# Modulation products on four 32-column strips of the array, partial rows added by a 128x2 matrix or by VectorE

## Chip, cores and metric

One core of one Trainium2 chip. The metric is device microseconds of one execution of the whole program.

## The reference

Two layers of one mixer block over 2048 latent tokens and 256 context tokens, width 1024. Each layer first makes its modulation: `silu(c) @ w_mod + b_mod`, with `w_mod` of 1024 x 3072, cut into shift, scale and gate; the same with `c_ctx` for the context tokens. Then

```
u = standardize(x) * (1 + scale) + shift
heads: latent attention (8), retention (4), gated convolution, all from u @ w_in
x_new = layer_norm(ALPHA * x + gate * (heads @ w_out))
```

Only the products with `w_mod` are touched here. They have two rows (`c` and `c_ctx`), so each is a (2 x 1024) by (1024 x n) product in plain fp32.

## The kernel before

The program writes its order out by hand: every engine call goes through a `Meter` (line 85, which is why the profile gives L85 nearly everywhere) that adds an estimated cost to that engine's planned time, `spent`. Background generators do their next piece when the planned time of PE has passed that of what they wait for (`wait`, line 124). `p_cost` (line 105) charges an fp32 matmul four cycles a column, but one cycle where its output has 32 rows; it was written so for the sums of the softmax denominators (`den_head`, line 1528), four matmuls with a 128x32 matrix of ones whose outputs lie in partitions 0, 32, 64 and 96 of one bank. So what the meter charges sets the order of the program in the stages run by generators; in the attention stage the work is hung on step numbers instead (`later`).

Each layer has three stages: the projections (`stage_in`, line 404), attention (`Attention.run`), and the output (`Output.run`). The attention loop has 576 steps (32 query blocks of 18 key tiles) of six matmuls of 512 columns: three for the scores, one for the maxima of a later block, two for probabilities times values; VectorE reduces the maxima and takes a difference per step, ScalarE makes an exponential and a copy, and GpSimd adds two tiles every second step.

A modulation product has these parts. `mod_load` (247) loads 1024 x n of `w_mod` in four transfers. `mod_mm` (252) runs eight matmuls, k = 0 to 7, with the 128x2 slice of `cT` as the stationary operand and n columns of `wm` moving, all accumulating in partitions 0 and 1 of one bank; each fp32 matmul appears in the trace as two passes. `mod_rows` (261) copies the two rows to SBUF by ScalarE, or for the gate adds the bias by VectorE and stores to `gate_s`. `mod_cols` (269) turns the rows of shift and scale into columns with one PE transpose per 128, and adds the bias.

The products are made in three places:

- **Start, layer 0** (line 1107 on): four products of 512 columns for shift and scale, one after the other with their copies and transposes. Unit 0 (256 tokens) cannot be modulated before the fourth. The generators `gen_x` (standardize units of x), `gen_w` (split weights in two parts) and `gen_u` (modulate and split a unit) are stepped between them.
- **Attention, layer 0** (lines 1603 to 1625): twelve products of 256 columns, one per 40 steps: four for layer 0's gate, eight for layer 1's shift and scale, the latter followed three steps later by `mod_cols`.
- **Change of layers** (`Start.gen_gate`, 391): four products of 256 columns for layer 1's gate, from tiles `wg`; then the second pool of the projection stage is laid over the memory of `wg` (line 414), and units of x are loaded into it. `gen_gate` of `stage_in` (555) adds the bias.

Of the kernel before, what the change touches and what calls it, by code (L numbers as in the profile page):

```python
# [10 lines left out]
F32 = mybir.dt.float32  # L11
F32R = mybir.dt.float32r
I32 = mybir.dt.int32
AF = mybir.ActivationFunctionType
ALU = mybir.AluOpType
AX = mybir.AxisListType
# [3 lines left out]
D = 1024  # L20
# [53 lines left out]
def tile_hybrid(ctx: ExitStack, tc: tile.TileContext, I: dict, out: bass.AP, stop: str = ""):  # L74
    nc = tc.nc
# [41 lines left out]
    V, S, G = Meter(nc.vector, v_cost), Meter(nc.scalar, s_cost), Meter(nc.gpsimd, g_cost)  # L117
    PE, SY = Meter(nc.tensor, p_cost), Meter(nc.sync, d_cost)
# [5 lines left out]
    def wait(*ms):  # L124
        at = max(m if isinstance(m, float) else m.spent for m in ms) + margin["engine"]
        if SY in ms or isinstance(ms[0], float):
            at += margin["dma"]
        yield
        while PE.spent < at:
            yield  # L130


    def pool(name, bufs=1, **kw):
        return tc.tile_pool(name=name, bufs=bufs, reuse_waits="tile", **kw)

    ctx.enter_context(tc.manual_schedule())
    const = ctx.enter_context(tc.tile_pool(name="const", bufs=1))
# [6 lines left out]
    tiny = Tiny()  # L144
# [14 lines left out]
    def ps_o():  # L159
        return next_bank("O", 6, 2)  # L160

    ident = const.tile([128, 128], F32, name="ident")
    make_identity(nc, ident)
    identr = const.tile([128, 128], F32R, name="identr")
    V.tensor_copy(identr, ident)
    ones32 = const.tile([128, 32], F32, name="ones32")
    V.memset(ones32, 1.0)
    idx = const.tile([128, 4], F32, name="idx")
# [2 lines left out]
    def transpose(o, i, n=128, f32r=False):  # L171
        PE.transpose(o, i, (identr if f32r else ident)[0:n, 0:n])
# [9 lines left out]
            V.scalar_tensor_tensor(r, t, 1.5, r, op0=ALU.add, op1=ALU.mult)  # L182
        return r

    cT = const.tile([128, 8, 2], F32, name="cT")
    t_pool = ctx.enter_context(ExitStack())
    crow = t_pool.enter_context(pool("crow")).tile([16, 128], F32, name="crow")
    SY.dma_start(crow[0:8, :], I["c"].rearrange("b (k p) -> (b k) p", p=128))
# [1 line left out]
    if True:  # L190
        cps = ps_o()
        transpose(cps[:, 0:16], crow, 16)
        S.activation(cT.rearrange("p k j -> p j k"), cps[:, 0:16].rearrange("p (j k) -> p j k", j=2), AF.Silu)

    t_pool.close()
    x_s = dram.tile([T, D], F32, name="x_s")
# [8 lines left out]
    L = [dict() for _ in range(DEPTH)]  # L205
# [18 lines left out]
    def mod_params(l, prm):  # L224
        d = L[l]
        prmT = const.tile([128, NPRM], F32, name=f"prmT{l}")

        def rows(r, n, src):
            SY.dma_start(prm[r:r + n, :], src)

        rows(PB_MOD, 24, I["b_mod"][l].rearrange("(k p) -> k p", p=128))
        rows(PG_Q, 2, I["mla_q_norm"][l].rearrange("(k p) -> k p", p=128))
        rows(PG_KV, 1, I["mla_kv_norm"][l].rearrange("(k p) -> k p", p=128))
        rows(PDW, 62, I["conv_dw"][l].rearrange("t (k p) -> (t k) p", p=128))
        rows(PDW_B, 2, I["conv_dw_b"][l].rearrange("(k p) -> k p", p=128))
        rows(PLN_G, 2, I["conv_ln_g"][l].rearrange("(k p) -> k p", p=128))
        rows(PLN_B, 2, I["conv_ln_b"][l].rearrange("(k p) -> k p", p=128))
        rows(PPW_B, 2, I["conv_pw_b"][l].rearrange("(k p) -> k p", p=128))
        d["prm"] = prmT
        d["modc"] = const.tile([128, 16, 2], F32, name=f"modc{l}")  # L240

    def mod_flip(l, prm, p=None):
        p = ps_a() if p is None else p
        transpose(p[:, 0:NPRM], prm[0:NPRM, :], NPRM)
        V.tensor_copy(L[l]["prm"], p[:, 0:NPRM])

    def mod_load(l, c0, n, wm):
        for q in range(4):
            SY.dma_start(wm[:, 2 * q:2 * q + 2, 0:n], I["w_mod"][l, q * 256:(q + 1) * 256, c0:c0 + n]
                         .rearrange("(k p) c -> p k c", p=128))  # L250

    def mod_mm(l, c0, n, wm, ps):
        d = L[l]
        for k in range(8):
            PE.matmul(ps[0:2, 0:n], lhsT=cT[:, k, :], rhs=wm[:, k, 0:n], start=(k == 0), stop=(k == 7))

    def mod_bias(l, c0, n, row):
        if c0 >= 2 * D:
            SY.dma_start(row[:, 0:n], I["b_mod"][l:l + 1, c0:c0 + n].to_broadcast([2, n]))

    def mod_rows(l, c0, n, ps, row):
        if c0 < 2 * D:
            S.copy(row[:, 0:n], ps[0:2, 0:n])
        else:
            V.tensor_tensor(row[:, 0:n], ps[0:2, 0:n], row[:, 0:n], op=ALU.add)
            SY.dma_start(L[l]["gate_s"][:, c0 - 2 * D:c0 - 2 * D + n], row[:, 0:n])
        return row

    def mod_cols(l, c0, n, row, ps):
        d = L[l]  # L270
        nj = n // 128
        mv = ps[:, 0:2 * nj].rearrange("p (c j) -> p c j", j=2)
        for j in range(nj):
            transpose(mv[:, j, :], row[:, j * 128:(j + 1) * 128], 2)
        cs = slice(c0 // 128, c0 // 128 + nj)
        mo = d["modc"][:, cs, :]
        V.tensor_tensor(mo, mv, d["prm"][:, cs, None].to_broadcast([128, nj, 2]), op=ALU.add)
        if c0 >= D:
            V.tensor_scalar(mo, mo, 1.0, None, op0=ALU.add)
# [75 lines left out]
    class Start:  # L355
# [35 lines left out]
        def gen_gate(self, pend):  # L391
            for i in range(2):
                while pend or not (self.PB if i == 0 else self.PS).free:
                    yield
                ps = (self.PB if i == 0 else self.PS).take()
                for j in range(2):
                    c0 = 512 * i + 256 * j
                    mod_mm(self.l, 2 * D + c0, 256, self.wms[2 * i + j], ps[:, c0 % 512:c0 % 512 + 256])
                self.gates.append((512 * i, ps, self.PB if i == 0 else self.PS))
# [4 lines left out]
    def stage_in(l, only, pre):  # L404
# [13 lines left out]
        def slots(n, shape, name, dt=F32, p=keep):  # L418
            return Slots([p.tile(shape, dt, name=f"{name}{i}") for i in range(n)])
# [15 lines left out]
        T2 = slots(6, [128, 2, UN], "t")  # L435
# [118 lines left out]

        def gen_gate(c0, ps, home):
            rt = yield from T2.grab()
            row = rt[0:2].rearrange("p a b -> p (a b)")
            mod_bias(l, 2 * D + c0, 512, row)
            yield from wait(SY)
            mod_rows(l, 2 * D + c0, 512, ps, row)  # L560
            home.put(ps)
            yield from wait(SY)
            T2.put(rt)
# [532 lines left out]
        def idle():  # L1096
            PE.spent += 1000
            sync()
            bg.step()
            pump()  # L1100
# [8 lines left out]
        if l == 0:  # L1109
            with ExitStack() as tmp:  # L1110
                wmp = tmp.enter_context(pool("wm_first"))
                wms = [wmp.tile([128, 8, 512], F32, name=f"wm{i}") for i in range(4)]
                pt = T2.take()
                prm = pt.rearrange("p a b -> p (a b)")[:, 0:128]
                for i in range(4):
                    mod_load(0, i * 512, 512, wms[i])
                    if i == 0:
                        mod_params(0, prm)
                        PE.spent = SY.spent + DMA_LATENCY
                        bg.step()  # L1120
                bg.add(gen_w(wlist))
                bg.add(gen_u(pre.units))
                bg.step()
                rows = [None] * 4
                for i in range(5):
                    if i > 0:
                        mod_cols(0, (i - 1) * 512, 512, rows[i - 1], ps)
                        PB.put(ps)
                    if i < 4:
                        ps = PB.take()  # L1130
                        mod_mm(0, i * 512, 512, wms[i], ps)
                        if i == 0:
                            p = PB.take()
                            mod_flip(0, prm, p)
                            PB.put(p)
                            T2.put(pt)
                        rows[i] = mod_rows(0, i * 512, 512, ps, T2.free[i].rearrange("p a b -> p (a b)")[0:2])
                    idle()
            ready["mod"] = True
        else:  # L1140
            for a in pre.gates:
                bg.add(gen_gate(*a))
            bg.add(gen_w(wlist))
            bg.add(gen_u(pre.units))
# [167 lines left out]
    class Attention:  # L1312
# [96 lines left out]
        def run(self, outer):  # L1409
            l, d, its, state, last = self.l, self.d, self.its, self.state, self.last  # L1410
# [18 lines left out]
            start = {}  # L1429
# [175 lines left out]
            wms, rows = {}, {}  # L1605

            def mod_a(j):
                wms[j] = wmp.tile([128, 8, 256], F32, tag="wm", name="wm")
                mod_load(*mods[j], 256, wms[j])
                rows[j] = tiny.tile([2, 256], F32, tag="row", name="row")  # L1610
                mod_bias(*mods[j], 256, rows[j])

            def mod_b(j):
# [33 lines left out]
            for i in range(len(its)):  # L1647
# [9 lines left out]
                h, b = divmod(i, 4)  # L1657
# [34 lines left out]
            for n in range(-LA, tot):  # L1692
# [16 lines left out]
                if n >= 0:  # L1709
                    i, k = steps[n]  # L1710
# [562 lines left out]
```

## Time and profile before

| | |
|---|---|
| median of 3 runs | 3977.7 us (3975.3 to 3978.64) |
| the profiled execution | 3976.88 us |
| its span | 3974.8 us, granted TensorE clock 0.966 |
| PE, PEld | 93%, 78% of the span |
| VectorE (DVE), ScalarE (ACT), GpSimd (POOL) | 79%, 54%, 60% |

The span is cut out of an execution that took 2.1 us more. Busy shares are means over unlike stages, so the stage in which a product lies is looked at by itself. Overlapping matmuls count as busy PE once; what a group costs PE is read from the start of its first matmul to the start of the next that follows it.

### The profile page before, as it was taken

How to read it: one execution, taken by the hardware profiler on the slowest of the kernel's cores; microseconds unless marked ns; L12 is line 12 of the kernel's file. 1: busy time of each engine (PE TensorE's matmuls, PEld its weight loads, DVE VectorE, ACT ScalarE, POOL GpSimd, SP SyncE). 2: the span in 40 equal slices, each digit the busy share in tenths (PEclk: the TensorE clock that was granted, in tenths of full speed). 3: DMA queues.
4: the chain of work that ended last, by engine and by line, in shares of the span. 5: the costliest groups of instructions: out<-in, count | busy, mean ns of one | idle time of the engine just before them, and what ended most of it. 6: DMA issues, size and time to landing. Idle time of an engine off the chain costs nothing. (4 is left out here: it accounts for less than half of the span.)

```text
span 3974.8 us, 61355 instructions
## 1 busy us (share of the span) xinstructions
PE 3713.1 (93%) x21291; PEld 3106.9 (78%) x21291; DVE 3128.4 (79%) x6455; ACT 2141.5 (54%) x4090; POOL 2377.5 (60%) x1381
## 2 busy tenths in 40 slices
PE   7999988989999999989987999899899999999898
PEld 4999888967777777767767998898777777776676
DVE  4966937978888888868787659558798999998787
ACT  2342323257878877855323333222488888888332
POOL 2455345459988877733333454454499988887333
PEclk9999999989999999999998999999899999999999
DMA  4474543643332212055453653535522322111553
GB/s 155 126 218 118 159 146 105 191 113 83 75 82 63 70 45 53 22 143 161 139 172 104 184 160 115 179 98 175 146 52 60 72 57 50 39 30 44 143 159 109
DMA packets 413466, 438.57 MB, mean 110 GB/s; under 512 B 47850, under 2 KB 364380, under 8 KB 410980
## 3 DMA queue, kind: packets, MB, share of 16 engines
q1 hardware_dynamic: 413156, 434.67, 38.6%
q8 instruction: 167, 2.74, 0.3%
q14 instruction: 143, 1.17, 0.1%
HBM read 293.89 MB, written 140.67 MB: 109 GB/s over the span
## 5 line engine op out<-in xcount | busy, mean ns | idle before, releaser
L85 POOL TENSOR_TENSOR acc<-acc,ph 128x1024 f32<-128x1024 f32 x448 | 1060.5, 2367 | 121.7 <-ACT ph L85 99.2
L85 PE MATMUL bank<-qt,kt 96*128 96x512 f32 (+1 forms) x3456 | 1007.6, 400 | 8.6 <-DVE pl L85 7.3
L85 DVE TENSOR_REDUCE mx<-bank 128x1 f32<-128x512 f32 (+1 forms) x1152 | 787.0, 686 | 196.5 <-PE bank L85 139.8
L85 PEld LDWEIGHTS bank<-qt,kt 96*128 96x128 f32 (+1 forms) x3456 | 655.3, 191 | 229.3 <-issue 17.2
L85 DVE TENSOR_TENSOR pl<-bank,ph 128x512 fp32r<-128x512 f32 x1152 | 783.2, 680 | 28.4 <-ACT ph L85 22.7
L85 ACT ACTIVATE bank<-bank 128x512 f32<-128x512 f32 x1160 | 681.4, 587 | 87.7 <-PE bank L85 79.3
L85 ACT CAST ph<-bank 128x512 fp32r<-128x512 f32 x1152 | 674.7, 586 | 65.3 <-POOL acc L85 3.5
L85 PE MATMUL bank<-w,u 128*128 128x256 f32 (+1 forms) x4224 | 559.5, 290 | 9.1 <-POOL w L85 3.8
L85 PEld LDWEIGHTS bank<-w,u 128*128 128x128 f32 x4224 | 539.2, 193 | 13.6 <-POOL w L85 5.6
L85 PE MATMUL bank<-u,w 128*128 128x256 f32 x4080 | 524.2, 287 | 21.9 <-ACT w L85 9.8
L85 PEld LDWEIGHTS bank<-u,w 128*128 128x128 f32 x4080 | 505.6, 193 | 28.3 <-ACT w L85 10.2
L85 POOL TENSOR_TENSOR w<-x,w 128x512 fp32r<-128x512 f32 (+2 forms) x206 | 342.1, 1679 | 240.7 <-ACT w L85 220.8
L85 PE MATMUL bank<-kt,qt 96*128 96x512 f32 (+1 forms) x1280 | 463.3, 382 | 19.7 <-DMA kt<-k_s 14.4
L85 PE MATMUL bank<-ph,vt 128*128 128x512 f32 x1152 | 460.6, 400 | 1.6 <-ACT o L85 1.6
L85 DVE SCALAR_TENSOR_TENSOR ac<-wn,prmT,ac 128x384 f32<-128x384 f32 (+1 forms) x780 | 456.4, 656 | 0.0
L85 PE MATMUL bank<-pl,vt 128*65 128x512 f32 x1152 | 434.5, 395 | 6.6 <-DVE pl L85 5.5
L85 PE MATMUL bank<-wo,oh 128*128 128x512 f32 x1632 | 416.6, 408 | 9.7 <-DVE wraw L85 9.0
L85 PEld LDWEIGHTS bank<-wo,oh 128*128 128x128 f32 x1632 | 311.1, 196 | 78.7 <-DVE wraw L85 9.5
L85 PEld LDWEIGHTS bank<-kt,qt 96*128 96x128 f32 x1280 | 245.4, 192 | 86.3 <-issue 14.7
L85 POOL TENSOR_TENSOR t<-t,t 128x512 f32<-128x512 f32 x64 | 85.0, 1328 | 340.7 <-DVE t L85 249.5
L85 POOL TENSOR_TENSOR acc<-ph 128x1024 f32<-128x1024 f32 x64 | 151.4, 2366 | 204.3 <-ACT ph L85 200.4
L85 PEld LDWEIGHTS bank<-ph,vt 128*128 128x128 f32 x1152 | 217.2, 189 | 53.9 <-ACT o L85 12.8
(257 smaller groups left out, 4453.7 us busy)
## 6 DMA issues: line engine op xcount, KB each, us to landing
x<-in_w_in_dram SPq DMA_DIRECT2D x106, 512.0 KB
q_s<-so SPq DMA_DIRECT2D x102, 256.0 KB
k_s<-so SPq DMA_DIRECT2D x72, 256.0 KB
v_s<-so SPq DMA_DIRECT2D x36, 512.0 KB
kt<-k_s SPq DMA_DIRECT2D x32, 576.0 KB
vt<-v_s SPq DMA_DIRECT2D x48, 384.0 KB
ret_s<-t SPq DMA_DIRECT2D x70, 256.0 KB
qt<-q_s SPq DMA_DIRECT2D x64, 256.0 KB
```

Of the source, the lines that this page charges most:

```text
L85: return f(*a, **k)
```

## The change

```diff
+    identr = const.tile([128, 128], F32R, name="identr")
+    with ExitStack() as once:
+        eye = once.enter_context(pool("eye")).tile([128, 128], F32, name="eye")
+        make_identity(nc, eye)
+        V.tensor_copy(identr, eye)
+    ident = identr.bitcast(F32)
...
-    cT = const.tile([128, 8, 2], F32, name="cT")
+    cT = const.tile([128, 46], F32, name="cT")
+    V.memset(cT, 0.0)
+    fold = const.tile([128, 2], F32, name="fold")
+    V.tensor_reduce(fold, ident.rearrange("p (j c) -> p c j", c=32)[:, 0:2, :], axis=AX.X, op=ALU.add)
...
         for k in range(8):
-            PE.matmul(ps[0:2, 0:n], lhsT=cT[:, k, :], rhs=wm[:, k, 0:n], start=(k == 0), stop=(k == 7))
+            j = k % 4
+            PE.matmul(ps[32 * j:32 * j + 32, 0:n], lhsT=cT[:, 2 * k:2 * k + 32], rhs=wm[:, k, 0:n], start=(k < 4), stop=(k >= 4))
...
         if c0 < 2 * D:
-            S.copy(row[:, 0:n], ps[0:2, 0:n])
+            S.copy(row[:, 0:n], ps[:, 0:n])
         else:
-            V.tensor_tensor(row[:, 0:n], ps[0:2, 0:n], row[:, 0:n], op=ALU.add)
-            SY.dma_start(L[l]["gate_s"][:, c0 - 2 * D:c0 - 2 * D + n], row[:, 0:n])
+            for j in range(4):
+                V.tensor_tensor(row[0:2, 0:n], ps[32 * j:32 * j + 2, 0:n], row[0:2, 0:n], op=ALU.add)
+            SY.dma_start(L[l]["gate_s"][:, c0 - 2 * D:c0 - 2 * D + n], row[0:2, 0:n])
...
-            transpose(mv[:, j, :], row[:, j * 128:(j + 1) * 128], 2)
+            PE.matmul(mv[:, j, :], lhsT=row[:, j * 128:(j + 1) * 128], rhs=fold, start=True, stop=True)
```

Products k and k + 4 go to strip k % 4 of the array, that is to partitions 32j to 32j + 31 of the bank. The stationary operand is 32 columns wide: the two of this k, and after them those of later k or zeros, so that rows 2 to 31 of a strip hold values that nobody wants. `fold` has a one at partitions 0, 32, 64, 96 in its first column and at 1, 33, 65, 97 in its second: a matmul with it as the moving operand picks the eight good rows, adds the four strips and turns them into columns at once. For the gate four VectorE adds do that. The tiles that hold the rows have all 128 partitions now. The fp32 identity becomes a view of the rounded one, and its own tile a short-lived one. The meter's rule for 32 output rows now also takes `mod_mm`, so that a product is planned at a quarter of its former cost.

## Rows read from the trace of the kernel before

**Rows 1.** Busy time by stretch: stretch, its length, busy us of each engine, granted clock, DMA share, GB/s.

```profile
0.00:50.00 50.00, 35.70 (x102) 10.08 (x102) 15.41 (x52) 5.78 (x11) 0.95 (x7) 1.00 0.70 255
860.00:1660.00 800.00, 798.61 (x3565) 589.11 (x3564) 692.50 (x1130) 645.20 (x1160) 671.00 (x342) 1.00 0.25 61
940.00:980.00 40.00, 40.00 (x180) 28.39 (x179) 33.26 (x54) 31.36 (x57) 38.51 (x24) 1.00 0.38 87
2040.00:2140.00 100.00, 74.01 (x408) 58.97 (x407) 69.75 (x177) 33.77 (x66) 29.89 (x19) 0.84 0.48 153
```

**Rows 2.** Groups of PE matmuls by shape: the products of the attention stage.

```profile
L85 PE MATMUL bank<-wm,cT 128*2 128x256 f32 x192 | 43.4, 379 | 0.0
```

**Rows 3.** Timeline, PE: one product of the attention stage (start us, us).

```profile
1152.97 0.40 PE L85 MATMUL bank<-pl,vt 128*65 128x512 f32 x1
1153.30 3.62 PE L85 MATMUL bank<-wm,cT 128*2 128x256 f32 x16
1156.84 0.96 PE L85 MATMUL bank<-qt,kt 97*128 97x512 f32 x3
```

**Rows 4.** Timeline, PE: the four denominator sums of one head.

```profile
953.26 0.39 PE L85 MATMUL bank<-pl,vt 128*65 128x512 f32 x1
953.57 0.63 PE L85 MATMUL bank<-da,ones 128*32 128x512 f32 x3
...
954.03 0.60 PE L85 MATMUL bank<-da,ones 128*32 128x512 f32 x3
...
954.57 0.73 PE L85 MATMUL bank<-qt,kt 97*128 97x512 f32 x2
```

**Rows 5.** Instructions on the gate's row tile, VectorE (ns min/median/max).

```profile
L85 DVE TENSOR_TENSOR row<-bank,row x4: 411/412/413, 912.6 to 1096.5; 2x256 f32<-2x256 f32 x4
```

**Rows 6.** Timeline, PE: two transposes of a row; full-height fp32 matmuls of 64 columns.

```profile
1161.60 0.28 PE L85 MATMUL bank<-ident,row 2*128 2x2 f32 x2
1161.82 0.97 PE L85 MATMUL bank<-qt,kt 97*128 97x512 f32 x3
...
1721.67 0.39 PE L85 MATMUL bank<-r_st,qT 128*128 128x64 f32 x2
1721.89 0.39 PE L85 MATMUL bank<-rr,am 128*128 128x64 f32 x2
```

**Rows 7.** Timeline of the start.

```profile
1.19 0.36 SPq L85 DMA_DIRECT2D crow<-in_c_dram  x1
...
1.33 0.29 DVE L85 CAST identr<-ident 128x128 fp32r<-128x128 f32 x1 [1.33 <-POOL ident masks.py:199]
...
15.14 8.67 PE L85 MATMUL bank<-wm,cT 128*2 128x512 f32 x16
...
33.27 1.29 DVE L85 BATCH_NORM_STATS2 bs<-so 128x6 f32<-128x512 f32 x2
...
49.45 2.80 ACT L85 ACTIVATE t<-bank,modc 128x256 f32<-128x256 f32 x6
...
52.71 1.08 PE L85 MATMUL bank<-u,w 128*128 128x256 f32 x7
...
63.36 13.97 POOL L85 TENSOR_TENSOR u<-t,u 128x512 fp32r<-128x512 f32 x8 [5.89 <-DVE u L85]
```

**Rows 8.** DMA rates from 0 to 60 us in 40 slices of 1.5 us.

```profile
GB/s 0 31 265 396 324 340 396 351 34 40 339 393 396 396 388 386 389 389 381 389 399 404 382 348 381 407 128 11 0 0 0 0 0 5 165 381 153 0 0 0
```

**Rows 9.** Timeline of the change of layers.

```profile
2069.16 14.31 PE L85 MATMUL bank<-wg,cT 128*2 128x256 f32 x64
...
2080.05 0.79 SPq L85 DMA_DIRECT2D so<-x_s  x2
...
2090.03 0.45 PE L85 MATMUL bank<-ident,so 128*128 128x128 f32 x1 [6.55 <-DVE so L85]
...
2091.12 1.27 DVE L85 TENSOR_TENSOR t<-bank,t 2x512 f32<-2x512 f32 x2
```

**Rows 10.** Waits of SP's queue from 2050 to 2095 us: us, times, longest.

```profile
SPq L85 <- PE bank L85: 4.0, 1, 4.0
```

More of the change, by code (lines that the diff above doesn't have):

```diff
@@ L160, in ps_o @@
         return next_bank("O", 6, 2)
-    ident = const.tile([128, 128], F32, name="ident")
-    make_identity(nc, ident)
     identr = const.tile([128, 128], F32R, name="identr")
-    V.tensor_copy(identr, ident)
+    with ExitStack() as once:
[3 more added lines that the diff above has]
+    ident = identr.bitcast(F32)
     ones32 = const.tile([128, 32], F32, name="ones32")
@@ L192, in tile_hybrid @@
         transpose(cps[:, 0:16], crow, 16)
-        S.activation(cT.rearrange("p k j -> p j k"), cps[:, 0:16].rearrange("p (j k) -> p j k", j=2), AF.Silu)
+        S.activation(cT[:, 0:16].rearrange("p (k j) -> p j k", j=2), cps[:, 0:16].rearrange("p (j k) -> p j k", j=2), AF.Silu)
     t_pool.close()
@@ L254, in mod_mm @@
         for k in range(8):
-            PE.matmul(ps[0:2, 0:n], lhsT=cT[:, k, :], rhs=wm[:, k, 0:n], start=(k == 0), stop=(k == 7))
+            j = k % 4
+            PE.matmul(ps[32 * j:32 * j + 32, 0:n], lhsT=cT[:, 2 * k:2 * k + 32], rhs=wm[:, k, 0:n], start=(k < 4), stop=(k >= 4))
     def mod_bias(l, c0, n, row):
         if c0 >= 2 * D:
-            SY.dma_start(row[:, 0:n], I["b_mod"][l:l + 1, c0:c0 + n].to_broadcast([2, n]))
+            SY.dma_start(row[0:2, 0:n], I["b_mod"][l:l + 1, c0:c0 + n].to_broadcast([2, n]))
     def mod_rows(l, c0, n, ps, row):
         if c0 < 2 * D:
-            S.copy(row[:, 0:n], ps[0:2, 0:n])
+            S.copy(row[:, 0:n], ps[:, 0:n])
         else:
-            V.tensor_tensor(row[:, 0:n], ps[0:2, 0:n], row[:, 0:n], op=ALU.add)
-            SY.dma_start(L[l]["gate_s"][:, c0 - 2 * D:c0 - 2 * D + n], row[:, 0:n])
+            for j in range(4):
+                V.tensor_tensor(row[0:2, 0:n], ps[32 * j:32 * j + 2, 0:n], row[0:2, 0:n], op=ALU.add)
+            SY.dma_start(L[l]["gate_s"][:, c0 - 2 * D:c0 - 2 * D + n], row[0:2, 0:n])
         return row
@@ L556, in gen_gate @@
             rt = yield from T2.grab()
-            row = rt[0:2].rearrange("p a b -> p (a b)")
+            row = rt.rearrange("p a b -> p (a b)")
             mod_bias(l, 2 * D + c0, 512, row)
@@ L1136, in stage_in @@
                             T2.put(pt)
-                        rows[i] = mod_rows(0, i * 512, 512, ps, T2.free[i].rearrange("p a b -> p (a b)")[0:2])
+                        rows[i] = mod_rows(0, i * 512, 512, ps, T2.free[i].rearrange("p a b -> p (a b)"))
                     idle()
@@ L1609, in mod_a @@
                 mod_load(*mods[j], 256, wms[j])
-                rows[j] = tiny.tile([2, 256], F32, tag="row", name="row")
+                rows[j] = tiny.tile([128, 256], F32, tag="row", name="row")
                 mod_bias(*mods[j], 256, rows[j])
```

## The prediction

> **What bounds the kernel now.** I read the busy time by stretch first, because the products lie in three places that need not have the same limit. In layer 0's attention (860 to 1660 us) PE is busy 798.6 of 800 us at the full granted clock; VectorE is busy 692.5 (87%), GpSimd 671 (84%) [rows 1]. There a microsecond taken from PE is a microsecond of the run, as long as no other engine fills up. GpSimd comes closest: 38.5 of 40 us in 940:980, where the retention scan runs beside the sums [rows 1]. At the start PE is busy 35.7 of the first 50 us and VectorE 15.4, so the order of arrivals and waits counts, not one engine. At the change of layers (2040 to 2140) PE is busy 74% and no engine is full [rows 1].
>
> Next the groups by shape. The twelve products of the attention stage are 192 records of 256 columns, two passes for each of 96 matmuls [rows 2]. Last the timelines, for what one product holds PE up: the busy figure counts overlaps once, so I take start to start.
>
> **Attention: the products.** One product starts at 1153.30 and the next score matmul at 1156.84: 3.54 us for 16 passes, 0.221 each [rows 3]. Will four strips run side by side? The trace holds the same form already: the denominator sums are four fp32 matmuls, 128x32 stationary, on the four strips of one bank, 512 columns each. Their first passes start together at 953.57, the second passes at 954.03, and the next score matmul at 954.57: 1.00 us for as many columns as a product has (4 x 512 = 8 x 256) [rows 4]. One after another, at the 0.221 us per 256 columns of [rows 3], they would have taken 16 x 0.221 = 3.54. The lead-in is the same in both, 0.33 and 0.31 us from the start of the matmul ahead [rows 3, 4]. So a product falls from 3.54 to 1.00, by 2.54, and twelve by **30.5 us**. A product has twice as many weight loads as the sums, which could cost some tenths: I keep 1.00 to 1.3, that is 27 to 30.5.
>
> The skill speaks against a gain of that size: the Trainium skill, TensorEngine Tiling (Array Packing), Key Properties, says that a change of tiling mode drains the array. Were that new here, and worth the 0.3 us of lead-in at each end, twelve products would give back about 7 us. Rows 3 and 4 show the same lead-in for the 2-column products of before as for 32-column strips, so I take it as paid already.
>
> **Attention: what is added.** (a) `mod_cols`: two transposes of a row hold PE 0.22 us (1161.60 to 1161.82). A full-height fp32 matmul of few columns takes 0.22 by itself (1721.67 to 1721.89) [rows 6], so the pair with `fold` takes 0.44, and the eight of them add 8 x 0.22 = 1.8. (b) The gate's rows: four adds for one, of 0.411 us [rows 5], 1.23 more on VectorE four times, 4.9 us together. VectorE has 13% to spare, about 8 us in the 61 us between two products, and the maxima and differences queued behind the adds are needed a step or more later; so nothing, and if that cover is gone, 4.9. (c) ScalarE's copy of 128 partitions instead of 2 has the same number of elements each: nothing, hidden behind PE; without that cover at most eight times a part of one copy. (d) GpSimd, 96% busy while the scan runs, gets 2.5 us less per 61 us for the same work in the two or three products that fall there: about 1 us lost, at most 3 x 2.5. Sum: -30.5 + 1.8 + 1 = **-28**, between -30 and -15 with every bound taken.
>
> **Start.** The four products are followed by the first modulation at 49.45, and the first projection matmul at 52.71 [rows 7]. The first product runs from 15.14 [rows 7]. Four of 512 columns at four times the speed would leave PE waiting for data instead: transfers go at some 390 GB/s from 15 us on [rows 8]. The last three tiles of `w_mod` are 6.3 MB, so the last is there at 15 + 6.3/0.39 = 31 us; with its product (about 2), copy and fold the first modulation can begin at about 35 rather than 49.45. That is a ceiling of **-14**. Against it stands the order. `p_cost` charges a product here 8 x 512 x 4 / 2.4 ns = 6.8 us before and 1.7 after, which takes 20 us out of the planned time of the loop, so the generators that wait for planned transfers are not served inside it any more: the standardization of unit 1, which now starts at 33.27 beside the third product [rows 7], and the first splitting of `w_in` move behind unit 0's modulation. The standardization's 9 us on VectorE were free there and then are not. What really comes last here is GpSimd's splitting of units 1 and 2, 13.97 us from 63.36, which waited 5.89 us for VectorE [rows 7]; it comes forward by less than unit 0 does. I take half of the ceiling, **-7**, with +8 (one standardization exposed in full) and -14 as ends. The DMA queue SP gets one wait: if `crow` is laid over the short-lived identity, its load (now issued at 1.19) waits for the cast that ends at 1.62 [rows 7], and x and `w_mod` are queued behind it: +0.5, in that half.
>
> **Change of layers.** The four gate products run from 2069.16 for 14.3 us [rows 9]; in strips they take 4. But the next PE work waits for something else: the transposes of a unit at 2090.03, after 6.55 us idle [rows 9]. The loads of that unit, issued at 2080.05, had waited 4.0 us for PE, since they go over the memory of `wg` [rows 9, 10]. So 4 of the 10 us come through. Given back: VectorE's two bias adds of 512 columns (1.27 us for both [rows 9]) become eight, +3.8, in front of modulation work. Sum about 0; again the planned time is shorter against the queues', which moves unit 0's projection ahead of the next unit's transposes: I take **-1**, from -8 to +8.
>
> The kernel has no products after that, and in layer 1's attention nothing changes. The order of the projection stages may change in detail; what that does is in the ends above.
>
> **Sum.** -28 - 7 - 1 = -36 on the profiled execution of 3976.9 us, which is 0.8 us from the median shown: **3941 us**.
>
> **Rivals.**
>
> *Strips in turn (slower).* If the passes on different strips did not overlap, a product would still take 16 x 0.221 = 3.54 us. Then nothing is gained, and the additions stand: 1.8 for `fold`, 3.8 for the bias adds at the change of layers, 0.5 for `crow`, some 2 for adds in attention: 3977 + 8 = 3985. It decides at the second matmul: whether it starts before the first has ended. Rows 4 speak against it plainly; for it only that a product has eight weight sets and not four.
>
> *The vector side sets the pace.* GpSimd at 96% and VectorE at 87% fill up when PE's pauses of 3.54 us, in which they catch up, are gone. Price: 7.5 us for GpSimd in the scan, 4.9 for the adds in attention, and the 3.8 of the change of layers not offset by the earlier loads: -36 + 16 = -20, 3957. For it speaks 38.5 of 40; against it that this is one stretch of 800 us.
> The Trainium skill, TensorEngine Tiling (Array Packing), PSUM Bottleneck, has that rule: tiling speeds up the products, not the emptying of PSUM, and the copy can become the bottleneck. For the gate it would be so by the rows, 4 x 0.411 = 1.64 us of adds against a product of 1.00, but once in 61 us.
>
> *The new order is worse.* The standardizations come late in both places, +8 at the start and +8 at the change of layers: -28 + 16 = -12, 3965.
>
> *The new order is better.* The start takes its whole ceiling and the change of layers 8: -28 - 14 - 8 = -50, 3927.
>
> **How the numbers follow.** Forecast 0.60 (its own range 3929 to 3953), vector side 0.10, worse order 0.13, better order 0.13, strips in turn 0.04. The range of 3920 to 3963 takes in the forecast, the better order, the vector side and most of the worse order; left out are strips in turn and the tail of the orders. A change of 0.2% is 8 us, about what a measurement can tell from none. All cases but strips in turn lie beyond it on the fast side, though a worse order than I price would fall inside: faster 0.94, same 0.03, slower 0.03.
>
> **What would show it.** In attention, a product of 16 passes in 1.0 to 1.3 us from start to start; eight records at a time in two starts each, and the twelve 40-step periods 2.3 us shorter. GpSimd and VectorE then up by some 3 points of busy share, PE still full. At the start, the first modulation at about 35 and `w_mod` transfers as the last release ahead of the later products; the standardization of unit 1 after unit 0's casts. At the change of layers, the loads at 2080.05 issued 4 us earlier after the gate products, and eight adds. I am wrong if a product takes over 2 us, if PE shows idle time in attention, if the first projection matmul comes no earlier, or if the 700 us of projections that follow change by more than 10 us.

## The result and the profile after

The changed kernel takes 3938.6 us in the median (3933.03 to 3947.03, 4 runs) against 3976.55 us for the kernel before (4 runs; the table above has 3 of them): a ratio of 0.9906 with a 95% interval of 0.9887 to 0.9924, or 38 us less. The forecast was 3941, in a range of 3920 to 3963. The execution whose profile follows is the slowest of the four, 3947.03 us with a span of 3945.2; a second profile of the same kernel (first experiment) has 3935.56.

In attention a product is now one group of 16 passes between two score matmuls. From the timeline of PE and VectorE, kernel after (start us, us):

```profile
1140.84 0.40 PE L85 MATMUL bank<-pl,vt 128*65 128x512 f32 x1
1141.17 1.07 PE L85 MATMUL bank<-wm,cT 128*32 128x256 f32 x16
1142.17 0.96 PE L85 MATMUL bank<-qt,kt 97*128 97x512 f32 x3
...
1146.81 0.50 PE L85 MATMUL bank<-fold,row 128*128 128x2 f32 x4
1147.17 0.94 PE L85 MATMUL bank<-qt,kt 97*128 97x512 f32 x3
...
907.14 1.78 DVE L85 TENSOR_TENSOR row<-bank,row 2x256 f32<-2x256 f32 x4 [0.21 <-PE bank L85]
```

From 1141.17 to 1142.17 is 1.00 us, where [rows 3] had 3.54, and the lead-in from the matmul ahead is 0.33 as it was. The pair with `fold` holds PE 0.36 us, where the transposes held it 0.22 [rows 6]. Busy time by stretch, kernel after, the stretches that answer to the second and third of [rows 1]:

```profile
856.00:1630.00 774.00, 772.23 (x3598) 583.95 (x3598) 700.46 (x1148) 648.65 (x1166) 673.33 (x343) 1.00 0.25 63
935.00:975.00 40.00, 40.00 (x189) 29.02 (x188) 35.97 (x61) 33.04 (x60) 38.51 (x24) 1.00 0.39 87
```

PE is still full; VectorE went from 87% to 700.46/774 = 90%, GpSimd from 84 to 87%, as forecast. For the length of the stretch I take two marks on either side of all twelve products, the first sum of probabilities by GpSimd and the last row turned to columns. From the groups on those tiles (ns min/median/max, first to last start), first before, then after:

```profile
L85 POOL TENSOR_TENSOR acc<-ph x64: 1269/2402/2417, 838.2 to 3662.6; 128x1024 f32<-128x1024 f32 x62, 128x512 f32<-128x512 f32 x2
L85 PE MATMUL bank<-ident,row x16: 195/208/219, 1161.6 to 1595.1; 2*128 2x2 f32 x16
```

```profile
L85 POOL TENSOR_TENSOR acc<-ph x64: 1266/2399/2417, 835.8 to 3629.4; 128x1024 f32<-128x1024 f32 x62, 128x512 f32<-128x512 f32 x2
L85 PE MATMUL bank<-fold,row x32: 165/251/272, 1146.8 to 1562.3; 128*128 128x2 f32 x32
```

Before, 1595.1 - 838.2 = 756.9; after, 1562.3 - 835.8 = 726.5: **30.4 us** from attention.

The start, kernel after, timeline (in brackets the idle time ahead and what ended it):

```profile
15.78 3.21 PE L85 MATMUL bank<-wm,cT 128*32 128x512 f32 x16
...
28.00 1.05 PE L85 MATMUL bank<-wm,cT 128*32 128x512 f32 x4 [0.31 <-DMA wm<-in_w_mod_dram]
...
33.39 0.19 PEld L85 LDWEIGHTS bank<-wm,cT 128*32 128x32 f32 x4 [1.17 <-DMA wm<-in_w_mod_dram]
...
35.84 3.76 ACT L85 ACTIVATE t<-bank,modc 128x256 f32<-128x256 f32 x8
...
41.07 1.27 DVE L85 BATCH_NORM_STATS2 bs<-so 128x6 f32<-128x512 f32 x2
...
51.09 6.63 PE L85 MATMUL bank<-u,w 128*128 128x256 f32 x48
...
59.88 9.49 POOL L85 TENSOR_TENSOR u<-t,u 128x512 fp32r<-128x512 f32 x5 [4.78 <-DVE u L85]
...
64.07 27.99 PE L85 MATMUL bank<-u,w 128*128 128x256 f32 x233 [0.44 <-POOL u L85]
```

The later products wait for `w_mod` (the third at 28.00, the fourth at 33.39), the first modulation comes at 35.84 instead of 49.45 [rows 7], and the projections run through from 64.07. In the kernel before, the same long run of projections begins here:

```profile
71.11 28.61 PE L85 MATMUL bank<-u,w 128*128 128x256 f32 x230
```

So 7.0 us are gained at that point. Four other executions with the same start (the changed kernel again and the last three experiments) have this run begin at 62.53 to 62.91, so the gain there is 7.0 to 8.6 us, and the profile above shows its lower end.

One thing stands in no term of the prediction. The granted clock in the profile after is 1.00 (2.4 GHz) up to 32 us and 0.50 (1.2 GHz) from 40 to 50 us; between the two PE has waited for `w_mod` and then, up to 47.25 us, 9.70 us for the standardization of the second unit. The kernel before, with product behind product, keeps 1.00. The 15 transposes from 47.98 us on take 3.46 us; 11 of the same kind from 59.52 us on, at 1.00, take 1.42. How much of the start's gain this takes was not measured. Busy time from 40 to 50 us, before and after (third number from the end: the granted clock), and the first of those transposes:

```profile
40.00:50.00 10.00, 8.79 (x32) 2.77 (x32) 1.97 (x8) 3.06 (x7) 0.00 (x0) 1.00 0.01 2
40.00:50.00 10.00, 2.50 (x11) 2.21 (x12) 9.48 (x25) 2.75 (x7) 3.49 (x3) 0.50 0.32 104
```

```profile
47.25 0.47 PE L85 MATMUL bank<-identr,so 128*128 128x128 f32 x1 [9.70 <-DVE so L85]
```

The change of layers, kernel after, timeline:

```profile
2039.35 2.91 PE L85 MATMUL bank<-wg,cT 128*32 128x256 f32 x44
2042.93 3.56 PE L85 MATMUL bank<-wg,cT 128*32 128x256 f32 x20 [0.67 <-DMA wg<-in_w_mod_dram]
2046.43 0.89 SPq L85 DMA_DIRECT2D so<-x_s  x2
2046.93 0.38 PE L85 MATMUL bank<-u,w 128*128 128x256 f32 x1 [0.45 <-DVE u L85]
...
2052.85 1.27 DVE L85 BATCH_NORM_STATS2 bs<-so 128x6 f32<-128x512 f32 x2
...
2059.70 5.71 DVE L85 TENSOR_TENSOR t<-bank,t 2x512 f32<-2x512 f32 x8
2062.56 3.13 SPq L85 DMA_DIRECT2D gate_s<-t  x2
2065.78 0.82 SPq L85 DMA_DIRECT2D so<-x_s  x2
...
2075.68 0.48 PE L85 MATMUL bank<-identr,so 128*128 128x128 f32 x1 [13.98 <-DVE so L85]
...
2081.16 4.04 PE L85 MATMUL bank<-u,w 128*128 128x256 f32 x32
```

PE is done with the gate products 7 us sooner after their start, and unit 1 (the first of this layer) is projected 7.6 us after that start. But the third unit's loads (2065.78) stand in SP's queue behind the gate's stores, and these wait for the eight adds; then PE stands idle for 13.98 us. For the same place before, three lines: the start of the second unit's standardization, the third unit's loads, and the projections behind its transposes (of these only the start is compared):

```profile
2083.66 1.29 DVE L85 BATCH_NORM_STATS2 bs<-so 128x6 f32<-128x512 f32 x2 [1.70 <-DMA so<-x_s]
...
2092.74 0.82 SPq L85 DMA_DIRECT2D so<-x_s  x2
...
2108.01 1.19 PE L85 MATMUL bank<-u,w 128*128 128x256 f32 x8
```

From the first gate product to those projections it is 2108.01 - 2069.16 = 38.85 us before and 2081.16 - 2039.35 = 41.81 after: 3.0 us **lost**. Two other executions with the same stage have 41.82 (the changed kernel again) and 41.85 (one add in attention). Not all of it lasts: from the first gate product to the first up-projection of this layer (the first matmul with `wuq`) it is 159.5 us before, and 161.7, 159.9 and 161.3 in these three, so 0.4 to 2.2 us more.

### The profile page after: what moved, and what is told of

The parts are those of the page before. It is cut to its first block, busy times and chain, and to the rows that moved or that the text cites. A ratio compares the mean times of both kernels' runs of the same rounds, so it can differ in the third digit from the quotient of the medians.

```text
span 3945.2 us, 61427 instructions
## 1 busy us (share of the span) xinstructions
PE 3672.2 (93%) x21323; PEld 3102.0 (79%) x21323; DVE 3138.1 (80%) x6475; ACT 2140.7 (54%) x4090; POOL 2367.7 (60%) x1381
```

## The experiments

**The changed kernel again.** No edit.

> The changed kernel once more, unaltered, to see which stretch differs between executions. Theory: 3938 us, within 8, and the gain of 30 in layer 0's attention (first product to last fold) the same within 1 us; what varies lies in the projection stages. Rival: the attention gain itself varies by several us, then the spread is in how the strips overlap.

Measured: 0.9906 (0.9893 to 0.9918), 3934.42 us. The attention stretch is 1551.6 - 825.2 = 726.4 us, against 726.5. The two profiles part in the projections of layer 0, between the first up-projection (matmul with `wuq`) and the first tile that GpSimd clears for attention. Busy time of that stretch before, after, and after again, the last three columns the granted clock, the DMA share and GB/s:

```profile
201.10:804.20 603.10, 561.04 (x4515) 550.91 (x4513) 424.81 (x1015) 183.53 (x379) 292.46 (x225) 0.98 0.52 158
```

```profile
193.50:801.70 608.20, 566.57 (x4511) 556.25 (x4509) 425.25 (x1014) 182.41 (x377) 287.14 (x225) 0.96 0.51 156
```

```profile
190.60:792.30 601.70, 564.47 (x4512) 554.41 (x4510) 425.24 (x1014) 183.44 (x380) 287.58 (x224) 0.97 0.52 159
```

The same work took 608.2 or 601.7 us, and the longer one had the lower clock. So 6.5 us of the 11.5 between the two executions lie there, in a part whose work the change does not touch, and another 2.9 lie before it (193.5 against 190.6). The clock alone does not order the three: the kernel before took 603.1 us at 0.98, more than the 601.7 at 0.97. Why the clock differs between two executions of one kernel was not looked into.

**Strips in attention only.** Products at the start and at the change of layers as before; the main part of the edit (`fold`, the wider `cT` and the rounded identity are taken over too):

```diff
+                for k in range(8):
+                    i = k % 4
+                    PE.matmul(ps[32 * i:32 * i + 32, 0:256], lhsT=cT[:, 2 * k:2 * k + 32], rhs=wm[:, k, 0:256],
+                              start=(k < 4), stop=(k >= 4))
+                    PE.spent += 3 * 256 / 2.4
```

> Strips, fold matrix and four adds in the twelve products of attention alone; start and change of layers as before, planned costs and order as before. Theory (PE's pauses in attention carry the gain): 28 us under the kernel before, 3949. Rival (the start and the change of layers carry it, and attention refills on VectorE or GpSimd): less than 15 under, 3962 or more.

Measured: 0.9931 (0.9918 to 0.9945), 27 us less than before; the attention stretch is 1564.7 - 837.5 = 727.2 us. So attention carries some three quarters of the gain, as the sum had it.

**Planned cost as before, in the changed kernel.** The order of all engines is then that of before:

```diff
             PE.matmul(ps[32 * j:32 * j + 32, 0:n], lhsT=cT[:, 2 * k:2 * k + 32], rhs=wm[:, k, 0:n], start=(k < 4), stop=(k >= 4))
+            PE.spent += 3 * n / 2.4
```

> The changed kernel with a product charged to the planned time as before (four cycles a column), so that the order of all engines is that of before. Theory (the new order costs half of the start's gain): the projection matmuls run through from 57 to 60 us in place of 64, and the whole is 3 to 8 us faster than the changed kernel. Rival (the order is neutral, GpSimd's splitting or the loads set that point): within 3 us of the changed kernel.

Measured: 0.9917 (0.9904 to 0.9930), not faster than the changed kernel's 0.9906. The theory fell, and its start shows why. Timeline of this kernel:

```profile
34.91 1.29 DVE L85 BATCH_NORM_STATS2 bs<-so 128x6 f32<-128x512 f32 x2 [10.38 <-DMA so<-in_x_dram]
...
37.78 0.62 ACT L85 CAST w<-x 128x512 fp32r<-128x512 f32 x1 [9.21 <-DMA x<-in_w_in_dram]
38.31 0.58 ACT L85 COPY t<-bank 128x512 f32<-128x512 f32 x1
...
42.14 2.85 ACT L85 ACTIVATE t<-bank,modc 128x256 f32<-128x256 f32 x6 [2.22 <-DVE modc L85]
...
56.57 14.01 POOL L85 TENSOR_TENSOR u<-t,u 128x512 fp32r<-128x512 f32 x8 [5.89 <-DVE u L85]
...
64.53 10.64 PE L85 MATMUL bank<-u,w 128*128 128x256 f32 x83
```

In the old order the last product's copy stands on ScalarE behind a cast that waits for `w_in` until 37.78, and its `modc` on VectorE behind the standardization; so the first modulation comes at 42.14, not 35.84. In the new order that is free and the standardization comes late instead (41.07). The long run of projections begins at 64.53, against 64.07 in the profile above and 62.53 to 62.91 in the four other executions with the new order: with strips the old order is 0.5 to 2.0 us later, not earlier.

**A quarter of the planned cost, in the kernel before.**

```diff
             PE.matmul(ps[0:2, 0:n], lhsT=cT[:, k, :], rhs=wm[:, k, 0:n], start=(k == 0), stop=(k == 7))
+            PE.spent -= 3 * n / 2.4
```

> The kernel before with a product charged a quarter, so that its order is that of the changed kernel while the products run as before. Theory: standardization of unit 1 exposed behind the first unit, 5 to 9 us at the start, so 3980 to 3986. Rival (the order is neutral or helps at the change of layers): 3970 to 3978.

Measured: 1.0012 (1.0004 to 1.0021), 3977.65 us, some 5 us more; the run of projections begins at 74.64 instead of 71.11, +3.5. The direction is the theory's; at the start the size is below its 5 to 9. The whole is within the theory's range only as a difference: 3977.65 itself lies in the rival's range, as the kernel before ran 3973.6 beside it and not 3977. The starts together: old order 71.11 without strips and 64.53 with them, new order 74.64, and 62.53 to 64.07 with strips. The new order costs 3.5 us with slow products and nothing with fast ones. At the change of layers, by the same mark as above, the new order is a little ahead: 2108.56 - 2070.46 = 38.10 here against 38.85, and 41.81 against 2069.84 - 2027.57 = 42.27 in the experiment before this one.

**All eight products on one strip.**

```diff
-            PE.matmul(ps[32 * j:32 * j + 32, 0:n], lhsT=cT[:, 2 * k:2 * k + 32], rhs=wm[:, k, 0:n], start=(k < 4), stop=(k >= 4))
+            PE.matmul(ps[0:32, 0:n], lhsT=cT[:, 2 * k:2 * k + 32], rhs=wm[:, k, 0:n], start=(k == 0), stop=(k == 7))
...
-            for j in range(4):
+            for j in range(1):
...
-            PE.matmul(mv[:, j, :], lhsT=row[:, j * 128:(j + 1) * 128], rhs=fold, start=True, stop=True)
+            PE.matmul(mv[:, j, :], lhsT=row[0:32, j * 128:(j + 1) * 128], rhs=fold[0:32], start=True, stop=True)
```

> All eight products of a modulation go to strip 0 with the same 32-column operands and the same order as the changed kernel; rows 0 to 31 are copied, one bias add. Theory (side by side is the gain): a product in attention takes 3.5 us again, the stretch from the first gate add to the last fold is as long as before within 2 us, and the whole is 3960 to 3977, as only the order and the shorter rows differ. Rival (32-column operands or the fold bring the gain): a product stays near 1 us, the whole near 3938.

Measured: 1.0022 (1.0013 to 1.0031), 0.0022 x 3972 = some 9 us more than before, so beyond the upper end given for it (its run of projections at the start begins at 78.58). In attention, timeline:

```profile
1160.30 3.64 PE L85 MATMUL bank<-wm,cT 128*32 128x256 f32 x16
1163.87 0.96 PE L85 MATMUL bank<-qt,kt 97*128 97x512 f32 x3
```

3.57 us for the same 16 passes with the same operands, and 1603.4 - 846.2 = 757.2 us for the stretch, against 756.9 before (by the marks of the expectation, first gate add to last fold, 683.5 against 682.5). That strips run side by side is the whole of the gain there.

**One add instead of four in attention.** `for j in range(4 if n == 512 else 1)`.

> The four gate products of attention add strip 0 alone to the bias, three of four adds left out, so layer 0's gate is not the reference's. Theory (the adds in attention are hidden): from the first gate add to the last fold less than 1.5 us shorter than in the changed kernel, the whole within its spread, 3930 to 3945. Rival (VectorE sets the pace): 4 to 5 us shorter there.

Measured: the stretch is 1553.5 - 827.0 = 726.5 us, as with four adds (from the first gate add to the last fold 655.1, against 655.2); the whole 0.9898 (0.9882 to 0.9914). The adds are hidden.

**One add instead of four at the change of layers.** `for j in range(4 if n == 256 else 1)`.

> The two gate additions at the change of layers add strip 0 alone, six of eight adds left out, so layer 1's gate is not the reference's. Theory (the six adds are on the path there: the gate store waits for them, and the third unit's loads are queued behind the store): the third unit's loads come 4 us earlier against the first wg matmul, the whole 3 to 5 us less than the changed kernel, some 3932. Rival (hidden): no change, 3938.

Measured: from the first gate product to the third unit's loads 2053.04 - 2031.22 = 21.82 us, against 2065.78 - 2039.35 = 26.43, so 4.6 sooner; to the projections behind it 2068.42 - 2031.22 = 37.20, against 41.81. The six adds are on the path there and cost 4.6 us. The whole, 0.9897 (0.9880 to 0.9913), does not tell it apart from the changed kernel.

**The gate held back.**

```diff
         def gen_gate(c0, ps, home):
+            while pre.units[2] in so_of:
+                yield
```

> The changed kernel, but the gate of layer 1 (bias load, eight adds, store) is held back until the third unit has been standardized and transposed; nothing else is altered. Theory (place, not price: the stores of the gate hold SP's queue, and with it the third unit's loads): those loads come 10 us or more earlier, PE's 14 us wait before the third unit's transposes shrinks to under 6, and the whole is 6 to 11 us less than the changed kernel, 3927 to 3932. Rival (another wait follows, such as the loads of w_in or GpSimd's splitting): within 3 us of the changed kernel.

Measured, from the timeline of this kernel:

```profile
2032.80 3.31 PE L85 MATMUL bank<-wg,cT 128*32 128x256 f32 x44
...
2042.88 1.09 SPq L85 DMA_DIRECT2D so<-x_s  x2
...
2058.51 1.27 DVE L85 BATCH_NORM_STATS2 bs<-so 128x6 f32<-128x512 f32 x2
...
2064.85 0.45 PE L85 MATMUL bank<-identr,so 128*128 128x128 f32 x1 [8.44 <-DVE so L85]
...
2070.59 10.22 PE L85 MATMUL bank<-u,w 128*128 128x256 f32 x84
```

The third unit's loads go out 10 us after the first gate product instead of 26, but its standardization starts at 2058.51 only: VectorE has the unit ahead of it to do. PE's wait falls from 13.98 to 8.44, not to under 6, and the projections behind it come at 37.79 instead of 41.81. So 4.0 us are gained there, between the 6 to 11 of the theory and the rival's 3: another wait followed, VectorE's. The whole is 0.9900 (0.9885 to 0.9914), which is not told apart from 0.9906; that this version beats the changed kernel is shown for that stretch alone.

## Why the prediction was right, point by point

- **A product from 3.54 to 1.00.** Right to the hundredth, and for the reason given: the denominator sums showed the form, and on one strip the time is back at 3.57. Twice as many weight sets cost nothing that shows. Twelve products are 30.5 us.
- **The drain on a change of mode.** No sign of a new cost: the lead-in is 0.33 us before and after.
- **`fold`, +1.8.** It was +1.1: a pair takes 0.36 us, not 0.44, so 8 x 0.14. The row taken for it had 64 columns, this has 2; that this is the reason was not tested.
- **Adds, copy and GpSimd in attention.** The adds are hidden, as said. GpSimd took back nothing of the 1 us I gave it, although it is as full as before (38.51 of 40). The measured terms give 30.5 - 1.1 = 29.4 and the stretch 30.4 to 30.5. The 1 us between goes with the planned cost: where it is as before, the stretch with strips is 727.2 (strips in attention only) and 1558.2 - 830.5 = 727.7 (planned cost as before), a gain of 29.2 to 29.7; a quarter of it in the kernel before makes 1596.1 - 839.8 = 756.3, 0.6 less than 756.9. By what way it acts in a stage that goes by step numbers was not looked into. The ends given for attention do not follow from their own terms, which make -30.5 + 1.8 = -28.7 and -27 + 1.8 + 4.9 + 7.5 = -12.8 instead of -30 and -15; the measured 30.4 lies just beyond the stated end.
- **Start, -7.** Right in size at the mark (7.0 to 8.6), wrong in its reason; half of a ceiling was taken without a sum, so that the size fits is luck. The first modulation at about 35 came at 35.84, held by the loads, as worked out, and `crow` was issued at 1.66 instead of 1.19, the 0.5 given. But the step "against it stands the order" failed: with the old order the start is no earlier. Its price was also too high: a standardization takes VectorE from 33.27 to 40.13, 6.9 us and not 9. What keeps the other half is, by the waits that the traces show, what the sentence on GpSimd said: the standardization, modulation and splitting of the second and third units, in either order.
- **Change of layers, -1.** It was +3 to the third unit's projections, within the ends given. Two steps were right: the loads over `wg` go out 2046.43 - 2039.35 = 7.1 us after the first product instead of 10.9 [rows 9], so 3.8 sooner; and the adds cost 5.71 - 1.27 = 4.4 more, with 4.6 seen on the path. The step that failed is "So 4 of the 10 us come through": the standardization behind those loads starts 2052.85 - 2039.35 = 13.5 us after the first product, against 2083.66 - 2069.16 = 14.5 before, so 1.0 came through. Before, VectorE waited for the loads (1.70 us); after, its line shows no wait, for VectorE was still busy with the first unit and its weights. Less 1.0 and plus 4.4 is +3.4, close to the +3.0 seen. "In strips they take 4" was wrong too: they took 7, as PE outran the loads of `wg`. And one wait was not named: the gate's stores wait for the adds, and the third unit's loads are queued behind them on SP. I had looked for what is queued behind the adds on VectorE and not behind the store.
- **The sum.** -30.4, -7.0 and +3.0 make -34.4 on the traces, against -36 forecast and -38 in the medians. That the sum fits is in part luck: attention gave 2.4 more than forecast, the change of layers 4 less. The span of the profiled execution is only 3974.8 - 3945.2 = 29.6 us shorter; its projections of layer 0, 608.2 us instead of 603.1, make +5.1 of the difference. The second profile of the same kernel is 3974.8 - 3933.1 = 41.7 shorter.
- **The rivals.** Strips in turn is excluded by the product of 1.00 us and by the one-strip kernel, which ran some 9 us slower than before by its ratio of 1.0022 (8 was given for that rival, though from other terms: this kernel has one bias add, and its run of projections at the start begins at 78.58 us against 71.11). The vector side is excluded in attention, by the length of the stretch and by the adds left out; its third part, the adds at the change of layers not offset by the earlier loads, came true. A worse order is excluded by the two kernels with exchanged order, a better one by 7.0 to 8.6 at the start, where it had 14, and by the loss at the change of layers. The worse order's 3965 lay outside the range that was said to take in most of it.

## What to carry to other kernels

Small products in fp32 with few rows can share the array by columns: sixteen passes took 1.00 us on four strips and 3.57 on one, and a matmul with a selection matrix adds the partial sums in the same step that turns rows to columns. The time is won only where PE is what everything waits for; in the two places with other limits, 16 and 8 us less of busy PE (29.75 to 13.67 us of products at the start, 14.31 to 6.04 at the change of layers) gave 7 and -3 at the marks used here. When a step gets more work on one engine, look for the store that waits for it and for the loads that are queued behind that store.

## What the runs showed of the hardware that was not expected

Sixteen passes with eight different sets of weights ran on four strips in 1.00 us, the same as eight passes with four equal sets did in the kernel before, so the extra weight loads hid completely; by the trace each of them takes at least 105 ns, 1.7 us for the sixteen. And one program had 608.2 and 601.7 us for the same 600 us of projections in two executions, at granted clocks of 0.96 and 0.97, a difference of 6.5 us, which is about as much as the whole effect of the start.
